# A convolution stage with its last phased chunk moved from the seventh to the eighth, no diagonal taps, and low weight parts formed by accumulating transfers

## The chip, the cores and the metric

The kernel runs on one core of a Trainium2 chip. The core has a matrix engine (TensorE, PE in the profile), a vector engine (VectorE, DVE), a scalar engine (ScalarE, ACT), GpSimd (POOL) and SyncE (SP), which here only issues DMAs; 16 DMA engines move data between HBM and the on-chip memory. Each engine takes its instructions in order, and the instructions of different engines are tied by semaphores. The metric is the device time of one execution in microseconds (us); lower is better.

## The reference

Two layers work on x of 512 tokens by 1024 features. Layer 0 is a Conformer convolution, layer 1 differential attention; each is followed by a SwiGLU feed-forward block and a gated per-layer embedding. The change lies wholly in the convolution of layer 0:

```python
u = rms_norm(h, conv_norm_g[j])
...
a = x @ w_pw1 + b_pw1
u = a[..., :D_MODEL] * jax.nn.sigmoid(a[..., D_MODEL:])
u = lax.conv_general_dilated(u, dw_w[:, None, :], ...)  + dw_b     # 31 causal taps for each feature
u = jax.nn.silu(layer_norm(u, ln_g, ln_b))
return u @ w_pw2 + b_pw2
```

So: a product to 2048 features, a gate, 31 taps along time for each of 1024 features, a layer norm over the features, and a second product.

## The kernel before

**Layout.** Activations lie feature-major: 8 chunks (0 to 7) of 128 features on the partitions by 512 tokens. Products are made to near float32 precision from split operands: a value w is kept as a rounded high part (`hi`) and a low part (`lo` = w − hi), and each product is three matmuls of 128x512 (`mm3`, L183 to L185): low × high, high × low, high × high, in this order.

**Weights.** `weight()` fetches a raw tile of 128x1024 (512 KB, SP's queue, L166), ACT casts it to `hi` (`parts`, L171), and DVE or POOL subtracts to get `lo` (L173). There are two raw buffers and four each for `hi` and `lo`, so that two pairs of weights (gate and linear part of one chunk) fit; the cast of a pair waits until TensorE has finished with the pair two chunks earlier. The weights of chunks 0 and 1 are loaded by hand; those of chunks 2 to 7 come from the two `pairs.append` lines in the loop. Two more, `pw`, hold the weights of the embedding's projection.

**The chunk loop.** For each chunk c TensorE makes two products of 24 matmuls, `pg = half(wg)` and `pa = half(wa)`; DVE scales both by the row norm (L557, L559), ACT takes the sigmoid, and DVE multiplies (L563 or L575). Then come the taps, in one of two ways.

- *Direct* chunks (0, 2, 4, 7): ACT scales shifted copies and POOL adds them (L475, L476; `POOL_TAPS` of them), DVE does the rest as multiply-adds into a PSUM bank (L483 to L487), and both sums are added (L492). Chunk 7 also has an identity matmul and four taps on TensorE with diagonal blocks (L383, L384), added at L494.
- *Phased* chunks (1, 3, 5, 6): the gated input goes to DRAM and comes back with four token phases spread over the partitions (`phased_in`, `pi`: one transfer out, four in, L389 and L393). TensorE does the taps with 8 blocks from `diag` (L406, L412) as 64 matmuls of 128x128 (L422). The result is copied out of PSUM (L435), goes to DRAM and back (`phased_out`, `po`, L437 and L440), gets a remainder (L443) and is finished with the bias and a shift (L449).

**PSUM.** Four banks `mm`, two `sc` and two `tp`. The direct sums and the phased taps of the earlier chunks use `sc`.

**The layer norm.** `moments(c)` squares each finished chunk on ACT (L520) and adds the chunk and its square to two running sums (L523, L526), on POOL for chunks below 6 and on DVE after. `add_moments` turns both sums with TensorE transposes (L256) and reduces them; then come a power on POOL (L636), a spread over the rows, and for each chunk shift, scale, SiLU and a split into `z`. While these run, TensorE is given the eight projections of the embedding (`factor`), issued after the last tap. Then the second product starts (`linear`, L679 to L682).

**Order.** A planner lists the instructions of each engine from simulated times; `tc.issue_after(x)` holds an instruction behind another in that list. The queues run in the listed order whatever the true times are.

Of the kernel before, what the change touches and what calls it, by code (L numbers as in the profile page):

```python
# [49 lines left out]
WARM = 12  # L50
ALONE = (7,)
CUTS = 2


PE_TAPS = (0, 0, 0, 0, 0, 0, 0, 4)
POOL_TAPS = (10, 0, 13, 0, 13, 0, 0, 11)


PHASED = (1, 3, 5, 6)
BEHIND = (6,)  # L60
BEHIND_COPY = {5: -3, 9: -1}
NPH = 4
# [4 lines left out]
for _c in range(NC):  # L67
    if _c in PHASED:
        TAPS += [(_c, g, m) for g in range(NPH) for m in (0, 4)]
    else:  # L70
        TAPS += [(_c, j) for j in range(0, PE_TAPS[_c], 4)]

# [22 lines left out]
def trunk(ctx, tc, xT, pT, wts, diag, dww, vec, rel, lamv, out):  # L95
# [9 lines left out]
    def sb(shape, tag, bufs, dt=F32):  # L105
        uid[0] += 1
        return pool.tile(shape, dt, tag=tag, name=f"{tag}_{uid[0]}", bufs=bufs)
# [60 lines left out]
    def parts(w, cut, eng=V, after=None, behind=None):  # L168
        _, raw, hi, lo = w
        with tc.issue_after(behind.ins) if behind else nullcontext():  # L170
            last_cast[0] = A.copy(hi[:, cut], raw[:, cut])  # L171
        with tc.issue_after(after.ins) if after else nullcontext():
            eng.tensor_tensor(lo[:, cut], raw[:, cut], f(hi[:, cut]), ALU.subtract)  # L173
# [165 lines left out]
    phase_load = [None]  # L339
    late = []  # L340
    rb = None
# [29 lines left out]
    def pe_taps(c):  # L371

        acc = accs[c] = sc() if c < NC - 2 else mm()
        if c in PHASED:
            return phased_taps(c, acc)
        for j in range(PE_TAPS[c]):
            if j % 4 == 0:
                n = min(4, PE_TAPS[c] - j)
                dg = sb([P, 2, 4, P], "C5", 2)[:, 0]
                with tc.issue_after(outs[NC - 3].ins):  # L380
                    nc.sync.dma_start(dg[:, :n], diag[TAPS.index((c, j)), :, :n])
            if j == 0:
                T.matmul(acc, ident, shrow, start=True, stop=False)  # L383
            last_tap[0] = T.matmul(acc, dg[:, j % 4], ups[c][:, j : j + S], start=False, stop=(j == PE_TAPS[c] - 1))  # L384

# [12 lines left out]
    def phased_mats(c):  # L398
        i = TAPS.index((c, 0, 0))
        mats, k = [], 0  # L400
        for g in range(NPH):
            if g < (3 if c == NC - 2 else 2):
                two = []
                for m in range(2):
                    two.append(sb([P, 4, P], f"D{(i + k) % 6}", 1))
                    nc.sync.dma_start(two[m], diag[i + 2 * g + m])  # L406
                    k += 1
            else:
                both_ = sb([P, 2, 4, P], "C5", 2)
                two = both_[:, 0], both_[:, 1]  # L410
                for m in range(2):
                    nc.sync.dma_start(two[m], diag[i + 2 * g + m])  # L412
            mats.append(two)
        return mats
# [12 lines left out]
    def phased_out(c):  # L427

        o = big()
        both_ = sb([P, 2, S], f"B{c}", 1)  # L430
        n = NPH // 2 if c == NC - 2 else NPH
        ways = []
# [11 lines left out]
        y.append(both_[:, 0])  # L444

        def finish():
            if c >= NC - 3:
                more(V)
            return V.scalar_tensor_tensor(  # L449
                both_[:, 0].rearrange(tok, r=NPH), both_[:, 1].rearrange("p (r n) -> p n r", r=NPH), col("dw_b", c),  # L450
                shrow.rearrange(tok, r=NPH), ALU.add, ALU.add,
            )

        if c < NC - 3:
            more(G)
        late.append(finish)
        if c < NC - 3:
            late.pop()()

    def other_taps(c):  # L460
        if c in PHASED:
            return phased_out(c)
        up, acc = ups[c], accs[c]
        tap = lambda j: up[:, j : j + S]
        a, b = PE_TAPS[c], PE_TAPS[c] + POOL_TAPS[c]
        alone = c in ALONE
        pacc = wk()
        for j in range(a, b):
            if j == a:
                A.activation(pacc, tap(j), AF.Identity, scale=wt(c, j), bias=col("dw_b", c))  # L470
            else:
                pr = sb([P, S], f"C{2 + j % 2}", 2)
                behind = [m for m in BEHIND_COPY if m <= j - a] if alone else []
                with tc.issue_after(copies[BEHIND_COPY[behind[-1]]].ins) if behind else nullcontext():
                    A.activation(pr, tap(j), AF.Copy, scale=wt(c, j))  # L475
                last_pool[0] = G.tensor_tensor(pacc, pacc, pr, ALU.add)  # L476
        yc = sb([P, 2, S], f"B{c}", 1)
        if c == 0:
            sums["acc"] = yc[:, 1]
        yc = yc[:, 0]  # L480
        sum_ = sc() if alone else acc
        if c == 0 or alone:
            V.tensor_scalar(sum_, tap(b), wt(c, b), None, ALU.mult)  # L483
        else:
            V.scalar_tensor_tensor(sum_, tap(b), wt(c, b), shrow, ALU.mult, ALU.add)
        for j in range(b + 1, KW):
            last_sum = V.scalar_tensor_tensor(sum_, tap(j), wt(c, j), sum_, ALU.mult, ALU.add)  # L487
            if c == NC - 1 and j == b + 12:
                with tc.issue_after(last_sum.ins):
                    late.pop(0)()  # L490
        with tc.issue_after(last_sum.ins) if alone else nullcontext():
            last_add[0] = V.tensor_tensor(yc, sum_, pacc, ALU.add)  # L492
        if alone:
            last_add[0] = V.tensor_tensor(yc, acc, yc, ALU.add)  # L494
        y.append(yc)
# [6 lines left out]
    last_moment = [None]  # L502
    last_add = [None]
    last_sum = [None]
    last_square = [None]
    last_mean = [None]
    copies = []
    last_pool = [None]

    def moments(c):  # L510
# [7 lines left out]
        sq = wk()  # L518
        with tc.issue_after(last_out[0].ins) if c == NC - 3 else nullcontext():
            last_square[0] = A.activation(sq, y[c], AF.Square)  # L520
        eng = G if c < NC - 2 else V
        if c > 1:
# [12 lines left out]
    for c in range(NC):  # L535
        wa, wg = pairs[c]
        if c == 0:
            pg, pa = first_halves(wa, wg)
            norm.factors()
            rb = norm.rows()  # L540
            pairs.append((weight(), weight())[::-1])
            pair_loads.append(loaded[0])
            ph = pfeatures(0, [(sb([P, S], t, 2, F32R), sb([P, S], t, 2, F32R)) for t in ("wth", "wtl")], norm.spread)
        if 1 < c < NC - 1:
            pairs.append((weight(), weight(load_behind=phase_load[0] if c + 1 in BEHIND else None))[::-1])
            pair_loads.append(loaded[0])
# [29 lines left out]
        if c == NC - 1:  # L576
            other_taps(c - 2)
            pe_taps(c - 1)
        if c > 0 and c != NC - 2:
            other_taps(c - 1)  # L580
        if c == 1:
            moments(0)
        elif c > 3:
            moments(c - 3)
    pe_taps(NC - 1)
    other_taps(NC - 1)
    with tc.issue_after(last_pool[0].ins):
        moments(NC - 3)
    with tc.issue_after(last_square[0].ins):
        A.activation(sb([P, 8], "lam", 1), vt[:, :8], AF.Silu)  # L590
    with tc.issue_after(last_add[0].ins):
        last_add[0] = late.pop()()
    with tc.issue_after(last_add[0].ins):
        sq = moments(NC - 1)
        V.scalar_tensor_tensor(sums["acc"], sq, NC * EPS, sums["acc"], ALU.add, ALU.add)
        moments(NC - 2)

# [25 lines left out]

    pw = [weight(eng=G), weight(eng=G)]
    vs = sb([P, P // 2], "v8", 2)[:, :12]
    for m in range(4):
        factor(last_tap, bank=(mm, mm, mm, sc)[m])
    factor(last_product, copied, between=add_moments)
# [17 lines left out]
    with tc.manual_schedule(engines={V.engine, A.engine}):  # L646
        for c in range(NC + 1):
            if c < NC:
# [5 lines left out]
                z_hi.append(A.copy(z[c][0], y[c]))  # L654
                if c < 3:
                    copied.pop()()
                if c < 2:
                    factor(last_product, copied, (sc, mm)[c])
            if c >= 1:
# [34 lines left out]
    def add_conv(m, acc):  # L694
# [4 lines left out]
        {"eng": G},  # L699
        {"behind": last_square[0], "after": last_pow[0], "eng": G, "load_behind": backs[NC - 2]},  # L700
        {"behind": last_square[0], "after": scaled[1], "load_behind": backs[NC - 2]},
    )
# [550 lines left out]
def _layout(a):  # L1253
# [43 lines left out]
    f = np.arange(FG)  # L1297
    for i, (c, *at) in enumerate(TAPS):
        if c not in PHASED:
            for k in range(min(4, PE_TAPS[c] - at[0])):  # L1300
                diag[i, np.arange(P), k, np.arange(P)] = dw[at[0] + k, c]
            continue
        g0, m0 = at
        for k in range(4):
# [46 lines left out]
```

## Time and profile before

| | us |
|---|---|
| median of 3 runs | 1224.14 |
| lowest, highest | 1223.39, 1225.11 |
| the profiled execution | 1225.47 |
| its span, first to last instruction | 1223.7 |

The profile shows one execution. "Busy" is the time in which an engine had an instruction running; matmuls are pipelined, so that their rows overlap, and a busy TensorE is not one at its peak. A row of the timeline has start, length, engine, line and tiles; a bracket gives the idle time before it and what ended it. The line of a helper such as `mm3` or `parts` stands for many uses. Numbered chunks in the text go from 0 to 7, so that the "eighth chunk" is chunk 7.

### The profile page before, as it was taken

What the parts mean: (1) busy time and instruction counts of PE and PEld (TensorE: products, weight loads), DVE (VectorE), ACT (ScalarE), POOL (GpSimd) and SP (SyncE); (2) the same over time, 40 slices, a digit from 0 to 9 for tenths busy, and PEclk for the clock granted to TensorE, in tenths of its full rate; (3) what the DMA queues carried; (4) which work ended last, traced back from release to release, by engine and by line L of the source; (5) the groups of instructions that cost most, each with busy time, mean ns of one, the idle gap of its engine ahead of it and who ended that gap; (6) DMA issues with size and microseconds to landing.
All of it is one profiled execution on the core that took longest, in us unless ns stands there. A gap on an engine that the chain in (4) does not pass through costs nothing.

```text
span 1223.7 us, 18446 instructions
## 1 busy us (share of the span) xinstructions
PE 1215.3 (99%) x7080; PEld 1072.7 (88%) x7080; DVE 897.1 (73%) x1442; ACT 623.2 (51%) x1039; POOL 279.3 (23%) x238
## 2 busy tenths in 40 slices
PE   9999999999999999999999999999999999999998
PEld 7888788898999899888888989888898999899887
DVE  6999957965698458668668879647865687568668
ACT  6764645432355235446566779635442355235443
POOL 0879421000000000042626544131000000000120
PEclk9999999999999999999999999999999999999999
DMA  8655232663567444243222214412654577353241
GB/s 285 216 177 157 93 121 71 187 165 111 125 170 185 141 106 123 84 145 96 76 92 78 78 55 128 138 59 79 182 163 122 136 173 190 105 138 94 78 139 69
DMA packets 60056, 156.96 MB, mean 128 GB/s; under 512 B 6336, under 2 KB 11200, under 8 KB 59968
## 3 DMA queue, kind: packets, MB, share of 16 engines
q1 hardware_dynamic: 53632, 136.20, 34.9%
q0 software_dynamic: 4608, 16.78, 8.3%
q10 hardware_dynamic: 1728, 2.80, 0.8%
q8 instruction: 55, 0.90, 0.3%
q14 instruction: 33, 0.27, 0.1%
HBM read 150.52 MB, written 4.19 MB: 126 GB/s over the span
## 4 chain that ended last, share of the span: by engine, by line
PE 88%; DVE 5%; DMA 3%; issue 1%; POOL 1%; ACT 1%; SPq 0%; DVEq 0%; POOLq 0%; ACTq 0%
PE mm L183 23%; PE mm L184 23%; PE mm L185 23%; PE tp L185 2%; PE tp L184 2%; PE tp L183 2%; PE sc L184 2%; PE sc L185 2%; PE sc L183 2%; PE mm L1119 1%; DVE wlo L173 1%; DMA C<-in_wts 1%; POOL wk L476 1%; DVE sc L487 1%; DMA wraw<-in_wts 1%
## 5 line engine op out<-in xcount | busy, mean ns | idle before, releaser
L183 PE MATMUL mm<-A,wlo 128*128 128x512 f32 (+1 forms) x816 | 277.0, 342 | 0.5 <-DVE wlo L775 0.5
L184 PE MATMUL mm<-A,whi 128*128 128x512 f32 (+1 forms) x816 | 276.8, 340 | 0.5 <-DVE A L198 0.5
L185 PE MATMUL mm<-A,whi 128*128 128x512 f32 (+1 forms) x816 | 276.9, 340 | 0.0
L171 ACT CAST whi<-wraw 128x1024 fp32r<-128x1024 f32 (+2 forms) x142 | 143.4, 1019 | 206.3 <-PE mm L185 88.1
L173 DVE TENSOR_TENSOR wlo<-wraw,whi 128x1024 fp32r<-128x1024 f32 (+2 forms) x135 | 171.7, 1275 | 54.5 <-ACT whi L171 54.4
L183 PEld LDWEIGHTS mm<-A,wlo 128*128 128x128 f32 x816 | 154.8, 190 | 18.1 <-PE sc L185 0.6
L184 PEld LDWEIGHTS mm<-A,whi 128*128 128x128 f32 x816 | 154.8, 190 | 17.7 <-DVE A L198 0.9
L185 PEld LDWEIGHTS mm<-A,whi 128*128 128x128 f32 x816 | 154.8, 190 | 16.6
L184 PE MATMUL mm<-B,whi 128*128 128x512 f32 (+1 forms) x384 | 147.5, 385 | 0.0
L185 PE MATMUL mm<-B,whi 128*128 128x512 f32 (+1 forms) x384 | 147.4, 385 | 0.0
L183 PE MATMUL mm<-B,wlo 128*128 128x512 f32 (+1 forms) x384 | 145.3, 386 | 0.0
L782 POOL DMA_DIRECT2D C<-in_wts x32 | 27.9, 873 | 506.3 <-DVE h L893 134.8
L224 POOL TENSOR_TENSOR acc<-acc,wk 128x512 f32<-128x512 f32 x34 | 55.8, 1640 | 215.3 <-ACT wk L222 107.4
L185 PEld LDWEIGHTS mm<-B,whi 128*128 128x128 f32 x384 | 72.1, 188 | 14.4
L183 PEld LDWEIGHTS mm<-B,wlo 128*128 128x128 f32 x384 | 72.2, 188 | 13.9
L184 PEld LDWEIGHTS mm<-B,whi 128*128 128x128 f32 x384 | 72.2, 188 | 13.7
L184 PE MATMUL mm<-wlo,A 128*128 128x512 f32 (+1 forms) x224 | 81.6, 367 | 0.0
L183 PE MATMUL mm<-whi,A 128*128 128x512 f32 (+1 forms) x224 | 80.9, 366 | 0.0
L185 PE MATMUL mm<-whi,A 128*128 128x512 f32 (+1 forms) x224 | 80.4, 362 | 0.0
L893 DVE TENSOR_TENSOR h<-mm,h 128x512 f32<-128x512 f32 x48 | 32.9, 687 | 63.5 <-PE mm L185 63.5
L250 POOL TENSOR_TENSOR r<-v,mhalf 128x8 f32<-128x8 f32 (+1 forms) x30 | 45.3, 1511 | 123.3 <-DVE v L248 122.5
L476 POOL TENSOR_TENSOR wk<-wk,C 128x512 f32<-128x512 f32 x43 | 63.4, 1479 | 13.5 <-ACT C L475 10.8
(322 smaller groups left out, 2749.6 us busy)
## 6 DMA issues: line engine op xcount, KB each, us to landing
wraw<-in_wts SPq DMA_DIRECT2D x161, 512.0 KB, 3.7
C<-in_wts SPq DMA_DIRECT2D x32, 512.0 KB, 4.5
C<-in_wts POOLq DMA_DIRECT2D x32, 512.0 KB, 6.0
bias<-in_wts SPq DMA_DIRECT2D x32, 256.0 KB, 3.3
wraw<-in_wts SPq DMA_DIRECT2D x16, 384.0 KB, 3.1
D<-in_diag SPq DMA_DIRECT2D x18, 256.0 KB, 4.9
C<-in_diag SPq DMA_DIRECT2D x15, 256.0 KB, 5.6
h<-in_xT SPq DMA_DIRECT2D x8, 256.0 KB, 5.2
```

The source lines that it names most:

```text
L171: last_cast[0] = A.copy(hi[:, cut], raw[:, cut])
L173: eng.tensor_tensor(lo[:, cut], raw[:, cut], f(hi[:, cut]), ALU.subtract)
L183: T.matmul(acc, al, bh, start=first, stop=False)
L184: T.matmul(acc, ah, bl, start=False, stop=False)
L185: return T.matmul(acc, ah, bh, start=False, stop=last)
L224: self.last = eng.tensor_tensor(self.acc, self.acc, sq, ALU.add)
L250: last_pow[0] = G.tensor_tensor(r[:, :n], v[:, :n], mhalf[:, :n], ALU.pow)
L476: last_pool[0] = G.tensor_tensor(pacc, pacc, pr, ALU.add)
L487: last_sum = V.scalar_tensor_tensor(sum_, tap(j), wt(c, j), sum_, ALU.mult, ALU.add)
L782: nc.gpsimd.dma_start(q, wts[i + 2].rearrange("p (a s) -> p a s", a=2), accum_op=ALU.add)
L893: V.tensor_tensor(h[m], acc, h[m], ALU.add)
L1119: T.matmul(o, wt[:, k * P : (k + 1) * P], val[hd, k], start=(k == 0), stop=(k == qb))
```

## The change

- The phased chunks are 1, 3, 5 and 7; chunk 6 becomes a direct one with 13 taps on ACT and POOL and 18 on DVE. No chunk has diagonal taps on TensorE.
- The weights of chunks 2 to 7 and the two `pw` weights get their low part in a new way (`eng=None`): ACT writes −hi into `lo`, and a DMA from POOL's queue adds the raw weight to it straight from HBM.
- POOL adds chunk 6 to the running sums. The calls at the end come in another order, five projections instead of four are issued straight after the last tap, and several hand-set orders go.

```diff
-ALONE = (7,)
...
-PE_TAPS = (0, 0, 0, 0, 0, 0, 0, 4)
-POOL_TAPS = (10, 0, 13, 0, 13, 0, 0, 11)
-PHASED = (1, 3, 5, 6)
+POOL_TAPS = (10, 0, 13, 0, 13, 0, 13, 0)
+PHASED = (1, 3, 5, 7)
...
     def parts(w, cut, eng=V, after=None, behind=None):
...
             last_cast[0] = A.copy(hi[:, cut], raw[:, cut])
+        if eng is None:
+            A.activation(lo[:, cut], hi[:, cut], AF.Copy, scale=-1.0)
+            nc.gpsimd.dma_start(lo[:, cut], wts[w[0], :, cut].bitcast(F32R), accum_op=ALU.add)
+            return
...
     def pe_taps(c):
-        acc = accs[c] = sc() if c < NC - 2 else mm()
+        acc = accs[c] = sc() if c < NC - 1 else mm()
         if c in PHASED:
-            return phased_taps(c, acc)
-        for j in range(PE_TAPS[c]):
...
-                T.matmul(acc, ident, shrow, start=True, stop=False)
-            last_tap[0] = T.matmul(acc, dg[:, j % 4], ups[c][:, j : j + S], start=False, stop=(j == PE_TAPS[c] - 1))
+            phased_taps(c, acc)
...
     def phased_out(c):
-        n = NPH // 2 if c == NC - 2 else NPH
+        n = NPH // 2 if c == NC - 1 else NPH
...
+        more(G if c < NC - 3 else V)
+        V.scalar_tensor_tensor(
+            both_[:, 0].rearrange(tok, r=NPH), both_[:, 1].rearrange("p (r n) -> p n r", r=NPH), col("dw_b", c),
+            shrow.rearrange(tok, r=NPH), ALU.add, ALU.add,
+        )
...
     def moments(c):
-        with tc.issue_after(last_out[0].ins) if c == NC - 3 else nullcontext():
+        with tc.issue_after(copies[-2].ins) if c == NC - 3 else nullcontext():
-        eng = G if c < NC - 2 else V
+        eng = G if c < NC - 1 else V
...
-            pairs.append((weight(), weight())[::-1])
+            pairs.append((weight(eng=None), weight(eng=None))[::-1])
...
-            pairs.append((weight(), weight(load_behind=phase_load[0] if c + 1 in BEHIND else None))[::-1])
+            pairs.append((weight(eng=None), weight(eng=None, load_behind=phase_load[0] if c + 1 in BEHIND else None))[::-1])
...
         if c == NC - 1:
             other_taps(c - 2)
-            pe_taps(c - 1)
...
+    moments(NC - 2)
     pe_taps(NC - 1)
     other_taps(NC - 1)
-    with tc.issue_after(last_pool[0].ins):
-        moments(NC - 3)
+    moments(NC - 3)
...
-    with tc.issue_after(last_add[0].ins):
-        last_add[0] = late.pop()()
-    with tc.issue_after(last_add[0].ins):
-        sq = moments(NC - 1)
-        V.scalar_tensor_tensor(sums["acc"], sq, NC * EPS, sums["acc"], ALU.add, ALU.add)
-        moments(NC - 2)
+    sq = moments(NC - 1)
+    V.scalar_tensor_tensor(sums["acc"], sq, NC * EPS, sums["acc"], ALU.add, ALU.add)
...
-    pw = [weight(eng=G), weight(eng=G)]
+    pw = [weight(eng=None), weight(eng=None)]
...
-    for m in range(4):
-        factor(last_tap, bank=(mm, mm, mm, sc)[m])
+    for m in range(5):
+        factor(last_tap, bank=(mm, mm, mm, sc, sc)[m])
...
-                if c < 3:
+                if c < 2:
                     copied.pop()()
-                if c < 2:
-                    factor(last_product, copied, (sc, mm)[c])
+                if c < 1:
+                    factor(last_product, copied, mm)
...
-        {"behind": last_square[0], "after": last_pow[0], "eng": G, "load_behind": backs[NC - 2]},
-        {"behind": last_square[0], "after": scaled[1], "load_behind": backs[NC - 2]},
+        {"behind": last_square[0], "after": last_pow[0], "eng": G, "load_behind": backs[NC - 1]},
+        {"behind": last_square[0], "after": scaled[1], "load_behind": backs[NC - 1]},
```

More of the change, by code (lines that the diff above doesn't have):

```diff
@@ L50 @@
 WARM = 12
-ALONE = (7,)
 CUTS = 2
-PE_TAPS = (0, 0, 0, 0, 0, 0, 0, 4)
-POOL_TAPS = (10, 0, 13, 0, 13, 0, 0, 11)
-PHASED = (1, 3, 5, 6)
+POOL_TAPS = (10, 0, 13, 0, 13, 0, 13, 0)
+PHASED = (1, 3, 5, 7)
 BEHIND = (6,)
-BEHIND_COPY = {5: -3, 9: -1}
 NPH = 4
@@ L69 @@
         TAPS += [(_c, g, m) for g in range(NPH) for m in (0, 4)]
-    else:
-        TAPS += [(_c, j) for j in range(0, PE_TAPS[_c], 4)]
 KDUP = "G"
@@ L339, in trunk @@
     phase_load = [None]
-    late = []
     rb = None
@@ L371, in pe_taps @@
     def pe_taps(c):
-        acc = accs[c] = sc() if c < NC - 2 else mm()
+        acc = accs[c] = sc() if c < NC - 1 else mm()
         if c in PHASED:
-            return phased_taps(c, acc)
-        for j in range(PE_TAPS[c]):
[L377 to L383, printed above, removed]
-            last_tap[0] = T.matmul(acc, dg[:, j % 4], ups[c][:, j : j + S], start=False, stop=(j == PE_TAPS[c] - 1))
+            phased_taps(c, acc)
     def phased_in(c, src):
@@ L401, in phased_mats @@
         for g in range(NPH):
-            if g < (3 if c == NC - 2 else 2):
+            if g < (3 if c == NC - 1 else 2):
                 two = []
@@ L444, in phased_out @@
         y.append(both_[:, 0])
[L446 to L458, printed above, removed]
+        more(G if c < NC - 3 else V)
[3 more added lines that the diff above has]
+        )
     def other_taps(c):
@@ L462, in other_taps @@
             return phased_out(c)
-        up, acc = ups[c], accs[c]
+        up, acc = ups[c], accs.get(c)
         tap = lambda j: up[:, j : j + S]
-        a, b = PE_TAPS[c], PE_TAPS[c] + POOL_TAPS[c]
-        alone = c in ALONE
+        b = POOL_TAPS[c]
         pacc = wk()
-        for j in range(a, b):
-            if j == a:
+        for j in range(b):
+            if j == 0:
                 A.activation(pacc, tap(j), AF.Identity, scale=wt(c, j), bias=col("dw_b", c))
@@ L472, in other_taps @@
                 pr = sb([P, S], f"C{2 + j % 2}", 2)
[L473 to L476, printed above, removed]
+                A.activation(pr, tap(j), AF.Copy, scale=wt(c, j))
+                G.tensor_tensor(pacc, pacc, pr, ALU.add)
         yc = sb([P, 2, S], f"B{c}", 1)
@@ L480, in other_taps @@
         yc = yc[:, 0]
-        sum_ = sc() if alone else acc
-        if c == 0 or alone:
-            V.tensor_scalar(sum_, tap(b), wt(c, b), None, ALU.mult)
+        if c == 0:
+            V.tensor_scalar(acc, tap(b), wt(c, b), None, ALU.mult)
         else:
-            V.scalar_tensor_tensor(sum_, tap(b), wt(c, b), shrow, ALU.mult, ALU.add)
+            V.scalar_tensor_tensor(acc, tap(b), wt(c, b), shrow, ALU.mult, ALU.add)
         for j in range(b + 1, KW):
[L487 to L494, printed above, removed]
+            V.scalar_tensor_tensor(acc, tap(j), wt(c, j), acc, ALU.mult, ALU.add)
+        V.tensor_tensor(yc, acc, pacc, ALU.add)
         y.append(yc)
@@ L502, in trunk @@
     last_moment = [None]
-    last_add = [None]
     last_sum = [None]
     last_square = [None]
+    copies = []
     last_mean = [None]
-    copies = []
-    last_pool = [None]
     def moments(c):
@@ L584, in trunk @@
             moments(c - 3)
+    moments(NC - 2)
     pe_taps(NC - 1)
     other_taps(NC - 1)
-    with tc.issue_after(last_pool[0].ins):
-        moments(NC - 3)
-    with tc.issue_after(last_square[0].ins):
+    moments(NC - 3)
+    with tc.issue_after(copies[-1].ins):
         A.activation(sb([P, 8], "lam", 1), vt[:, :8], AF.Silu)
-    with tc.issue_after(last_add[0].ins):
-        last_add[0] = late.pop()()
-    with tc.issue_after(last_add[0].ins):
-        sq = moments(NC - 1)
-        V.scalar_tensor_tensor(sums["acc"], sq, NC * EPS, sums["acc"], ALU.add, ALU.add)
-        moments(NC - 2)
+    sq = moments(NC - 1)
+    V.scalar_tensor_tensor(sums["acc"], sq, NC * EPS, sums["acc"], ALU.add, ALU.add)
     pp = []
@@ L1297, in _layout @@
     f = np.arange(FG)
[L1298 to L1303, printed above, removed]
+    for i, (c, g0, m0) in enumerate(TAPS):
         for k in range(4):
```

## The prediction

> **What bounds the kernel now.** I read the page's busy shares first, then TensorE's waits, then windows over the convolution, then the timeline of its end.
>
> ```profile
> span 1223.7 us, 18446 instructions
> PE 1215.3 (99%) x7080; PEld 1072.7 (88%) x7080; DVE 897.1 (73%) x1442; ACT 623.2 (51%) x1039; POOL 279.3 (23%) x238
> PE tp L256 <- DVE acc L523: 1.2, 1, 1.2
> 20.00:30.00 10.00, 10.00 (x48) 7.94 (x47) 5.23 (x8) 3.14 (x5) 1.18 (x2) 1.00 0.86 303
> 30.00:40.00 10.00, 9.99 (x45) 8.24 (x45) 9.96 (x13) 9.70 (x14) 5.51 (x5) 1.00 0.85 299
> 40.00:80.00 40.00, 40.00 (x241) 35.21 (x240) 39.29 (x43) 24.42 (x36) 32.91 (x24) 1.00 0.55 175
> 80.00:120.00 40.00, 40.00 (x221) 34.70 (x220) 39.22 (x52) 20.68 (x31) 36.88 (x27) 1.00 0.52 162
> ```
>
> The window columns are stretch, its length, then busy time of PE, weight load, DVE, ACT and POOL, granted clock (1.00), DMA share and GB/s. PE is never idle in the convolution's first 120 us, although DVE is full (39.3 of 40 us) and POOL nearly so: both run behind PE without holding it. PE's longest wait in the whole program is 1.2 us, for the transposes of the layer norm's sums. So PE's own work is the floor, and relief of DVE pays only where PE then waits less. The end of the convolution:
>
> ```profile
> 110.69 3.73 PE L422 MATMUL sc<-C,D 128*128 128x128 f32 x32
> 117.83 5.52 PE L422 MATMUL mm<-C,D 128*128 128x128 f32 x48
> 124.97 1.02 PE L383 MATMUL mm<-shrow,ident 128*128 128x512 f32 x2
> 128.87 0.80 PE L183 MATMUL mm<-wth,wlo 128*128 128x512 f32 x1
> 136.74 0.66 PE L256 MATMUL tp<-ident,acc 128*128 128x128 f32 x4 [1.16 <-DVE acc L523]
> 137.34 0.66 PE L256 MATMUL tp<-ident,B 128*128 128x128 f32 x4
> 143.59 0.39 PE L679 MATMUL mm<-A,whi 128*128 128x512 f32 x1
> 142.58 0.62 ACT L654 CAST A<-B 128x512 fp32r<-128x512 f32 x1
> ```
>
> Start, length, instruction. Chunks are numbered 0 to 7. PE ends chunk 7's products at 110.69, does chunk 5's phased taps (7.14 us), chunk 6's (117.83 to 124.97, 7.14 us), the identity and diagonal taps (124.97 to 128.87, 3.90 us), projections, the two groups of transposes, more projections, and the second pointwise product from 143.59. Its first operand's cast ends at 142.58 + 0.62 = 143.20.
>
> **The change, part by part.**
>
> *Removed from PE:* the identity and four diagonal taps, 3.90 us. With the 1.16 us wait that makes 5.06 us, the most this change can give while PE stays the floor.
>
> *The tail becomes a chain.* The projections follow the last tap in program order (they are issued after `last_tap`), and the last tap is now chunk 7's phased one, whose input goes to DRAM and back. Chunk 6 makes that trip now:
>
> ```profile
> 106.53 1.20 DVE L563 SCALAR_TENSOR_TENSOR big<-big,vec,big 128x512 f32<-128x512 f32 x1
> 107.75 0.34 SPq L389 DMA_DIRECT2D pi<-big  x1
> 109.75 1.74 SPq L393 DMA_DIRECT2D C<-pi  x4
> C<-pi SPq DMA_DIRECT2D x8, 64.0 KB, 2.0
> L559 DVE TENSOR_TENSOR big<-mm,rb 128x512 f32<-128x512 f32 x8 | 5.4, 680 | 0.0
> 125.18 0.65 ACT L435 COPY big<-mm 128x256 f32<-128x256 f32 x2 [2.23 <-PE mm L422]
> 127.28 1.75 SPq L440 DMA_DIRECT2D B<-po  x4
> B<-po SPq DMA_DIRECT2D x8, 64.0 KB, 1.9
> L443 DVE TENSOR_TENSOR B<-B,rest 128x240 f32<-128x240 f32 x2 | 2.3, 1154 | 0.0
> L449 DVE SCALAR_TENSOR_TENSOR B<-B,vec,shrow 128x512 f32<-128x512 f32 x4 | 5.1, 1282 | 0.0
> L520 ACT ACTIVATE wk<-B 128x512 f32<-128x512 f32 x7 | 4.3, 627 | 5.8 <-DVE B L449 3.2 <-DVE B L494 1.8 <-DVE B L492 0.7
> L595 DVE SCALAR_TENSOR_TENSOR B<-wk,B 128x512 f32<-128x512 f32 x1 | 0.7, 681 | 0.0
> ```
>
> From the end of the gated input (106.53 + 1.20 = 107.73) to the last landing: the fourth load starts at 109.75 + three quarters of 1.74 = 111.06, plus 2.0 gives 113.1, so 5.4 us. For chunk 7, from 110.69: L559 0.68, the gate 1.20, signals 0.2 (estimate), trip 5.4: 118.2. In between SP also issues the diagonal blocks for chunk 7, waiting for chunk 5's taps to free their buffers; I add 0.5 us (estimate; zero to 1.5, about the time of four such issues): 118.7. Chunk 5's taps, the only work left to PE, end at 117.83: **PE idles 0.9 us** where it did not. Taps: 118.7 + 7.14 = 125.8. Return: from 124.97 to the last landing (127.28 + 1.31 + 1.9 = 130.5) it is 5.5 us now, so 131.3. L443 1.15 and L449 1.28: 133.8. Square 0.63 with a signal (0.15), then L595 0.68: the second transposes start at 135.2, against 137.34. From there to the first operand's cast end it is 143.20 − 137.34 = 5.9 us: **product at 141.1–141.2 against 143.59, 2.4 us sooner.** PE's account agrees: 3.90 + 1.16 less, new idle of 0.9 ahead of the taps, some 0.9 ahead of the transposes and 0.6 ahead of the product: 2.7.
>
> *Moved to the direct way:* chunk 6 has 45 − 43 = 2 more POOL adds and two more DVE taps than chunk 7 had, less L494 and two of DVE's moment sums, which go to POOL. It starts two products of 5.46 us (below) before 110.69, at about 100, and need only be done before 133. I cost it at nothing. If POOL ended it after 127.5, the two sums of chunk 6 and then of chunk 5 (four POOL additions of some 1.5 us, L476's mean below, behind L492) would be later than the chain above.
>
> *Low parts of 14 weights.* DVE loses 12 subtractions and POOL two; ACT gains 14 casts, POOL 14 DMA issues:
>
> ```profile
> L173 DVE TENSOR_TENSOR wlo<-wraw,whi 128x1024 fp32r<-128x1024 f32 x10 | 17.7, 1768 | 0.0
> L476 POOL TENSOR_TENSOR wk<-wk,C 128x512 f32<-128x512 f32 x43 | 63.4, 1479 | 13.5 <-ACT C L475 10.8
> L171 ACT CAST whi<-wraw 128x1024 fp32r<-128x1024 f32 x14 | 14.6, 1041 | 4.9 <-DMA wraw<-in_wts 4.7
> L782 POOL DMA_DIRECT2D C<-in_wts x32 | 27.9, 873 | 506.3 <-DVE h L893 134.8
> q0 software_dynamic: 4608, 16.78, 8.3%
> 40.00:50.00 10.00, 10.00 (x71) 9.22 (x70) 9.96 (x10) 6.77 (x11) 9.61 (x7) 1.00 0.34 89
> C<-in_wts POOLq DMA_DIRECT2D x3, 512.0 KB, 8.4
> C<-in_wts POOLq DMA_DIRECT2D x32, 512.0 KB, 6.0
> 19.72 1.05 ACT L171 CAST whi<-wraw 128x1024 fp32r<-128x1024 f32 x1 [0.49 <-DMA wraw<-in_wts]
> 30.37 1.05 ACT L171 CAST whi<-wraw 128x1024 fp32r<-128x1024 f32 x1
> 30.04 0.49 PE L183 MATMUL mm<-A,wlo 128*128 128x512 f32 x1
> 77.95 0.48 PE L183 MATMUL mm<-A,wlo 128*128 128x512 f32 x1
> ```
>
> DVE gains 17.7 us in this stage and two subtractions before it; off PE's path that is worth nothing, except that DVE should then be prompt at 110.69, as the tail above assumes. ACT takes 14 × 1.04 = 14.6 us into a stage where it is busy 45 of 80 us. POOL takes 14 × 0.87 = 12.2 us, plus the adds and sums of chunk 6, less two subtractions; its queue is in order, so an issue that waits for ACT's second cast holds the L476 adds behind it, then ACT's scaled taps (their buffers) and DVE's last sum. PE has no direct need of these.
>
> The price lies in when the low part lands, because each product's first matmul reads it. The accumulating queue cost 8.3% × 1223.7 / 32 = 3.2 us of all 16 engines for each transfer. Four low parts (chunks 2 and 3) fall into 20–40 us, where DMA is at 0.86 and 0.85: 17.1 us used, 12.8 more wanted, 20 there. Later ones have 5 to 20 us to spare against a share near 0.55. The landing, 6.0 us in the median of the run, was 8.4 in the median of three at 225–246 us. Chunk 2's gate weight: cast ends 20.77, second cast 21.8, issue at 22.0, landed 30.4 by the 8.4, while PE wants it at 30.04. Chunk 3's: cast from 30.37, second cast ends 32.5, landed 40.9, wanted at 40.95 (two products after 30.04; the last six run from 77.95 to 110.69, so 5.46 us each). Both lie on the edge: **I take a stall of 0.8 us**, from 0 (landing of 8.0 or less) to 5 (13 us, all of the missing 10 us of DMA time shared between the two queues). A stall of the first shifts the second's need too, so they do not add.
>
> On this the Trainium skill can be weighed. Its page "DMA: Bandwidth & Descriptors", section "Anatomy of one DMA — SWDGE (gpsimd) path", gives about 2.0 us plus bytes over 436 GB/s for a transfer from this queue, by my estimate 3.2 us for 512 KB. By that the sum would have no stall; the rows here say 6.0 and 8.4, and I go by them. The same page, "Issuing engines are not separate DMA queues", says that transfers from all queues interleave on the same 16 engines, which speaks against this change: were the queues apart, the landing would stay at 6.0 and the stall at 0. No row here yet shows the early window overfull.
>
> *Sum:* 2.4 − 0.8 = 1.6 us sooner. The profiled execution took 1225.47 us, 1.77 around its span, and lies 1.33 above the median of 1224.14; the difference is carried to the median: **1222.5 us**.
>
> **Rivals.**
>
> 1. *Clean:* no stall, no time lost on SP's queue (0.5), and L449 falls from 1.28 towards the 0.68 that L595 takes for the same size (0.6). Gain 2.4 + 0.5 + 0.6 = 3.5, at most the floor of 5.06: about 1220.6. For it: DVE has slack and POOL has no subtraction left there until the power.
> 2. *Short landing:* the tail as forecast, but every low part lands in 8.0 us or less, as the run's median of 6.0 has it. The stall falls away: 1224.14 − 2.4 = 1221.7. This is also where the fixed price of the Trainium skill's page "DMA: Bandwidth & Descriptors" would lead.
> 3. *A bank:* the scratch banks in PSUM are two. Chunk 6's sum takes one earlier, so chunk 5's taps on PE wait for chunk 4's sum:
>
> ```profile
> 112.51 0.69 DVE L492 TENSOR_TENSOR B<-sc,wk 128x512 f32<-128x512 f32 x1
> ```
>
> It is read last at 112.51 + 0.69 = 113.2, now 2.5 us too late for 110.69. The relief of 17.7 us should bring it ten or more microseconds forward; if chunk 6's taps are put ahead of chunk 4's, it does not, and PE loses 2.5 to 7: about 1227.
>
> 4. *Slower, the early DMA window.* With DMA demand of 30 us in 20, the accumulates land after 12 to 14 us and the raw weights and diagonal blocks beside them are late too. The stall is landing − 8.0; it outweighs the 2.4 us from a landing of 10.4 us on, and by 0.2% from 12.9 on. At 13.5: 1224.14 − 2.4 + 5.5 = 1227.2. Against it: the window after it, 40–50 us, has a share of 0.34, so that what is not urgent can slip there.
>
> That the change doesn't do what it says is hardly open: five matmul groups go, and nothing else on PE is added.
>
> **How the numbers follow.** About 0.2%, 2.45 us, is what a measurement of this kernel can tell from no change. Forecast (gain 0.3 to 2.9): 0.45. Clean: 0.20. Short landing: 0.12, on the edge of 0.2%, half to each side. Bank: 0.08. Early DMA: 0.15. Faster: 0.20 + 0.06 + 0.07 of the forecast = 0.33. Slower: 0.08 + 0.15, and 0.01 of the forecast = 0.24. Same: the rest of the forecast, 0.37, and 0.06 = 0.43. The range for 8 in 10 goes from 1219.5, near the floor, to 1228.5, above both slower cases; the forecast's own is 1221.2 to 1223.8.
>
> **What would show it.** Right: no L383 and L384; PE idle for about 1 us ahead of the last L422 group, waiting for C<-pi; the second transposes 24.5 us after the end of chunk 7's products (26.65 now); L173 on DVE gone from 30–100 us; wlo landings of 8 us in 20–40 us with PE waiting at most a microsecond at the first L183 of chunk 2 or 3. Wrong: PE waiting several microseconds on a DMA before 60 us (rival 4); PE's chunk-5 taps waiting for L492 (rival 3); POOL's adds ending after 127 us, with the moment sums of POOL released last; or an order of instructions that moves chunk 5's taps ahead of chunk 7's products, so that nothing is left beside the trip.

## The result and the profile after

| | before | after |
|---|---|---|
| median, us | 1224.21 (5 runs) | 1243.55 (5 runs) |
| lowest, highest | 1223.39, 1225.11 | 1241.96, 1244.58 |
| ratio, 95% interval | | 1.0156 [1.0141, 1.017] |
| span of the profiled execution | 1223.7 | 1240.2 |
| mean granted clock | 1.000 | 0.993 |

The changed kernel is slower by 19.3 us in the median; the two profiled executions, 1225.47 and 1241.96 us, are 16.5 us apart, and the rows below account for these 16.5. The forecast was 1222.5, with a range up to 1228.5. Lines have moved: the casts are L166 and L168, the accumulating transfer L169, the matmuls of `mm3` L182 to L184, the phased taps L411, their way back L424 to L435, the running sums L491 and L494, the products' scaling and gate L525 to L531, and the second product L642.

The page of the changed kernel first (queue rows: packets, MB, share of 16 engines; issue rows: count, size, median us to landing):

```profile
PE 1220.2 (98%) x7070; PEld 1077.2 (87%) x7070; DVE 881.2 (71%) x1429; ACT 637.3 (51%) x1055; POOL 285.1 (23%) x254
q0 software_dynamic: 6624, 24.12, 11.6%
wlo<-in_wts POOLq DMA_DIRECT2D x14, 512.0 KB, 7.6
D<-in_diag SPq DMA_DIRECT2D x18, 256.0 KB, 7.6
C<-in_diag SPq DMA_DIRECT2D x14, 256.0 KB, 8.8
```

TensorE is still "98% busy" and even busier in microseconds (1220.2 against 1215.3) with ten instructions fewer; that share says nothing of where the time went. Where it went is in the windows and the timeline of the first 165 us. Windows of the changed kernel (columns as in the prediction):

```profile
20.00:30.00 10.00, 9.24 (x44) 7.10 (x43) 3.39 (x7) 7.55 (x10) 4.61 (x5) 1.00 0.99 294
30.00:40.00 10.00, 8.73 (x32) 7.07 (x33) 6.36 (x10) 6.64 (x10) 7.00 (x6) 0.83 1.05 298
40.00:50.00 10.00, 10.00 (x46) 8.29 (x45) 9.75 (x14) 10.00 (x15) 7.61 (x7) 1.00 0.96 292
50.00:60.00 10.00, 10.00 (x76) 9.19 (x75) 6.32 (x9) 7.33 (x11) 9.19 (x10) 1.00 1.03 262
```

The last column but one is the DMA share: full (about 1) for 40 us, where before it was 0.86, 0.85, in 40–50 0.34 and in 50–60 0.77. The column ahead of it is the granted clock: 0.83 in 30–40, where it was 1.00.

TensorE's timeline in the changed kernel (a bracket is the idle time before the row, and what ended it):

```profile
31.27 0.47 PE L182 MATMUL mm<-A,wlo 128*128 128x512 f32 x1 [2.03 <-DMA wlo<-in_wts]
32.67 0.63 PE L184 MATMUL mm<-A,whi 128*128 128x512 f32 x1
33.10 0.63 PE L182 MATMUL mm<-A,wlo 128*128 128x512 f32 x1
36.14 0.39 PE L184 MATMUL mm<-A,whi 128*128 128x512 f32 x1
36.37 0.39 PE L182 MATMUL mm<-A,wlo 128*128 128x512 f32 x1
...
78.71 5.44 PE L411 MATMUL sc<-C,D 128*128 128x128 f32 x32 [3.55 <-DMA C<-pi]
109.18 0.47 PE L182 MATMUL mm<-A,wlo 128*128 128x512 f32 x1 [1.01 <-DMA wlo<-in_wts]
116.75 0.47 PE L182 MATMUL mm<-A,wlo 128*128 128x512 f32 x1 [1.89 <-DMA wlo<-in_wts]
...
123.90 3.73 PE L411 MATMUL sc<-C,D 128*128 128x128 f32 x32
135.56 8.44 PE L411 MATMUL mm<-C,D 128*128 128x128 f32 x48 [4.36 <-DMA C<-pi]
145.54 0.48 PE L182 MATMUL mm<-wth,wlo 128*128 128x512 f32 x1
160.41 0.50 PE L642 MATMUL mm<-A,whi 128*128 128x512 f32 x1 [0.88 <-ACT A L617]
```

The second product starts at 160.41 instead of 143.59: 16.8 us, so the whole loss of the span (16.5) lies in the convolution stage. The projections start at 145.54 instead of 128.87, 16.7 us later, and behind them both kernels take the same (14.9 and 14.7). So the 16.7 us are to be found ahead of 145.54, and the rows give them:

- **Waits, 12.8 us**: 2.03 + 3.55 + 1.01 + 1.89 + 4.36.
- **A slow clock behind four of the five waits, 7.7 us.** At 32.67 one matmul follows the other after 0.43 us, at 36.14 after 0.23. That lasts some 3.4 us behind three of the waits and nearly 6 us behind the last. The 32 taps at 78.71 take 5.44 instead of 3.73 us; the last 64 taps take 145.54 − 135.56 = 10.0 instead of 7.14. The four cost 1.6, 1.7, 1.6 and 2.8 us.
- **Work removed, 3.9 us**: the diagonal taps are gone, as forecast. 12.8 + 7.7 − 3.9 = 16.6.

Why was chunk 7's input so late? Rows of the other engines in the changed kernel, in order of time (SPq rows are issues; L461 and L463 from 122.81 on are direct taps of chunk 6):

```profile
98.66 1.75 SPq L429 DMA_DIRECT2D B<-po  x4
103.47 2.97 DVE L435 SCALAR_TENSOR_TENSOR B<-B,vec,shrow 128x512 f32<-128x512 f32 x1 [7.55 <-POOL B L432]
115.42 0.72 ACT L526 ACTIVATE big<-big,vec 128x512 f32<-128x512 f32 x1 [3.93 <-DVE big L525]
117.44 0.88 POOL L169 DMA_DIRECT2D wlo<-in_wts  x1 [2.89 <-ACT wlo L168]
119.68 0.69 DVE L464 TENSOR_TENSOR B<-sc,wk 128x512 f32<-128x512 f32 x1 [4.29 <-POOL wk L453]
122.81 0.74 DVE L461 SCALAR_TENSOR_TENSOR sc<-C,C,shrow 128x512 f32<-128x512 f32 x1
123.59 3.13 DVE L463 SCALAR_TENSOR_TENSOR sc<-C,C,sc 128x512 f32<-128x512 f32 x4
126.63 0.68 DVE L527 TENSOR_TENSOR big<-mm,rb 128x512 f32<-128x512 f32 x1
128.32 1.57 DVE L531 SCALAR_TENSOR_TENSOR big<-big,vec,big 128x512 f32<-128x512 f32 x1 [0.35 <-ACT big L526]
129.92 0.33 SPq L378 DMA_DIRECT2D pi<-big  x1
```

Before, the same return of chunk 3 was issued here:

```profile
86.92 1.75 SPq L440 DMA_DIRECT2D B<-po  x4
```

Chunk 3's way back is 11.7 us late: its taps start 7.8 us later on TensorE (78.71 against 70.89), run slower, and their result takes 5.2 instead of 4.0 us to DRAM. DVE, which had been full, stands idle for 7.55 us with its list blocked by that one instruction. Then ACT waits for DVE, POOL's transfer for ACT's cast, and DVE for POOL's last add: each queue is in order, and the lateness goes around. It reaches TensorE too: the two low parts that it waits for at 109.18 and 116.75 belong to chunk 7 and are read 5.8 us after their issue, but they were issued only at 103.38 and 110.98, the first behind the late return in POOL's list. Chunk 7's products end at 123.90, its gate only at 128.32 + 1.57 = 129.9. That is 6.0 us later, where the prediction had 2.1. DVE is no longer idle then: it does chunk 6's taps, which stand in its list ahead of the last scaling (L527) and the gate (L531).

### The profile page after: what moved, and what is told of

Read it like the earlier page. It is cut to its first block, busy times and chain, and to the rows that moved or that the text cites. A ratio compares the mean times of both kernels' runs of the same rounds, so it can differ in the third digit from the quotient of the medians.

```text
span 1240.2 us, 18461 instructions
## 1 busy us (share of the span) xinstructions
PE 1220.2 (98%) x7070; PEld 1077.2 (87%) x7070; DVE 881.2 (71%) x1429; ACT 637.3 (51%) x1055; POOL 285.1 (23%) x254
## 3 DMA queue, kind: packets, MB, share of 16 engines
q0 software_dynamic: 6624, 24.12, 11.6%
## 4 chain that ended last, share of the span: by engine, by line
PE 91%; DMA 3%; DVE 2%; issue 1%; POOL 1%; ACT 1%; SPq 0%; ACTq 0%; DVEq 0%; POOLq 0%
PE mm L182 23%; PE mm L183 23%; PE mm L184 23%; PE tp L184 3%; PE tp L183 3%; PE tp L182 3%; PE sc L183 1%; PE sc L182 1%; PE sc L184 1%; PE mm L1082 1%; DMA D<-in_diag 1%; POOL wk L453 1%; PE sc L1049 1%; PE sc L411 1%; PE sc L1048 1%
## 5 line engine op out<-in xcount | busy, mean ns | idle before, releaser
L182 PE MATMUL mm<-A,wlo 128*128 128x512 f32 (+1 forms) x816 | 277.9, 343 | 5.2 <-DMA wlo<-in_wts 4.9
L184 PE MATMUL mm<-A,whi 128*128 128x512 f32 (+1 forms) x816 | 278.2, 341 | 0.0
L166 ACT CAST whi<-wraw 128x1024 fp32r<-128x1024 f32 (+2 forms) x142 | 143.4, 1018 | 210.0 <-PE mm L184 85.4
L172 DVE TENSOR_TENSOR wlo<-wraw,whi 128x1024 fp32r<-128x1024 f32 (+2 forms) x123 | 151.1, 1232 | 52.2 <-ACT whi L166 52.2
L182 PEld LDWEIGHTS mm<-A,wlo 128*128 128x128 f32 x816 | 155.6, 191 | 23.9 <-DVE big L527 2.4
L184 PEld LDWEIGHTS mm<-A,whi 128*128 128x128 f32 x816 | 155.7, 191 | 17.0
L184 PE MATMUL mm<-B,whi 128*128 128x512 f32 (+1 forms) x384 | 147.4, 385 | 0.0
L182 PE MATMUL mm<-B,wlo 128*128 128x512 f32 (+1 forms) x384 | 145.3, 386 | 0.0
L184 PEld LDWEIGHTS mm<-B,whi 128*128 128x128 f32 x384 | 72.2, 188 | 14.4
L182 PEld LDWEIGHTS mm<-B,wlo 128*128 128x128 f32 x384 | 72.2, 188 | 13.9
L183 PEld LDWEIGHTS mm<-B,whi 128*128 128x128 f32 x384 | 72.2, 188 | 13.8
L182 PE MATMUL mm<-whi,A 128*128 128x512 f32 (+1 forms) x224 | 80.9, 366 | 0.0
L184 PE MATMUL mm<-whi,A 128*128 128x512 f32 (+1 forms) x224 | 80.4, 362 | 0.0
```

What stands on the lines that cost most here:

```text
L182: T.matmul(acc, al, bh, start=first, stop=False)
L183: T.matmul(acc, ah, bl, start=False, stop=False)
L184: return T.matmul(acc, ah, bh, start=False, stop=last)
```

## The experiments

The change has two halves: where the chunks go (phased eighth chunk, no diagonal taps) and how low parts are made. Theory: an overfull DMA in 20–60 us, made by the accumulating transfers, gives the loss. Rival: the new tail loses by itself, with chunk 7's gate behind DVE's taps. Each kernel below computes the whole reference. A difference in us is the ratio's, on 1224 us. In the cuts of code, `...` stands for further lines of the edit.

### Each half by itself

The changed kernel with all low parts subtracted as before:

```diff
-pairs.append((weight(eng=None), weight(eng=None))[::-1])
+pairs.append((weight(), weight())[::-1])          # the second pairs line likewise
-pw = [weight(eng=None), weight(eng=None)]
+pw = [weight(eng=G), weight(eng=G)]
```

> The changed kernel, but all low parts made as before (DVE, and POOL for the two pw weights); the eighth chunk stays phased. Theory D (the 14 accumulating transfers overfill the DMA engines between 20 and 60 us, and everything that crosses DRAM comes late): DMA share back to 0.85 at 30-40 us, no PE wait for wlo, time 1221 to 1227, near the forecast tail's 1221.7. Theory T (the tail: the eighth chunk's trip through DRAM has too little work beside it): PE still waits over 4 us for C<-pi ahead of the last taps, time 1236 or more. Theory A (the extra casts on ACT hold its queue): as D.

Measured: 1235.09 us, 1.0079 [1.0063, 1.0096]. It waits nowhere for a low part. A window of it, TensorE's waits (total, times, longest), and the timeline of DVE and TensorE:

```profile
40.00:60.00 20.00, 20.00 (x123) 17.77 (x121) 19.61 (x24) 12.93 (x19) 19.33 (x14) 1.00 0.58 183
```

```profile
PE mm L411 <- DMA C<-pi: 9.6, 1, 9.6
PE tp L255 <- DVE acc L491: 1.4, 1, 1.4
```

```profile
113.12 2.41 DVE L461 SCALAR_TENSOR_TENSOR sc<-C,C,shrow 128x512 f32<-128x512 f32 x1
115.56 2.34 DVE L463 SCALAR_TENSOR_TENSOR sc<-C,C,sc 128x512 f32<-128x512 f32 x3
119.06 2.15 DVE L531 SCALAR_TENSOR_TENSOR big<-big,vec,big 128x512 f32<-128x512 f32 x1
...
109.77 3.73 PE L411 MATMUL sc<-C,D 128*128 128x128 f32 x32
126.71 8.23 PE L411 MATMUL mm<-C,D 128*128 128x128 f32 x48 [9.64 <-DMA C<-pi]
```

In 40–60 us the DMA is at 0.58 and the clock full, TensorE ends chunk 7's products at 109.77 without a wait, and still 9.7 us are lost: DVE is full, chunk 6's taps stand ahead of chunk 7's gate, and the gate ends at 121.2, 11.4 us after the products. The rival is true too.

The kernel before with the accumulating low parts in all 14 places (`eng=None` at both `pairs` lines and at `pw`):

```diff
         last_cast[0] = A.copy(hi[:, cut], raw[:, cut])
+        if eng is None:
+            A.activation(lo[:, cut], hi[:, cut], AF.Copy, scale=-1.0)
+            nc.gpsimd.dma_start(lo[:, cut], wts[w[0], :, cut].bitcast(F32R), accum_op=ALU.add)
+            return
...
```

> The kernel before, with the 14 low parts made by the sign-turned cast and the accumulating transfer; the seventh chunk stays phased and the diagonal taps stay. Theory D: DMA share near 1 at 20-60 us, PE waits for wlo and C<-pi, 1235 to 1245. Theory T: within 2 us of 1224. Theory A: 1235 or more, with PE's waits led by ACT and not by DMA.

Measured: 1244.24 us, 1.0161 [1.0146, 1.0176]. TensorE's waits in it (total, times, longest):

```profile
PE sc L426 <- DMA C<-pi: 4.2, 1, 4.2
PE mm L187 <- DMA wlo<-in_wts: 3.9, 3, 2.6
PE mm L426 <- DMA C<-in_diag: 3.4, 1, 3.4
PE mm L187 <- DVE big L563: 2.3, 1, 2.3
```

With the old tail the transfers alone cost as much as the whole change. So each half loses alone, 20 and 10 us, and together they lose 19: they share their waits and do not add. Only 3.9 of the 13.8 us of waits are put down to low parts; 7.6 are for the input of a phased chunk and for diagonal blocks, which had been in time before.

### Is it ACT's work or the transfer's, and its source?

The changed kernel, where DVE adds the raw weight to ACT's sign-turned cast, and no transfer is made:

```diff
-nc.gpsimd.dma_start(lo[:, cut], wts[w[0], :, cut].bitcast(F32R), accum_op=ALU.add)
+V.tensor_tensor(lo[:, cut], raw[:, cut], f(lo[:, cut]), ALU.add)
```

> The changed kernel with the sign-turned cast on ACT kept for the 14 low parts, but the raw weight added to it by DVE from the raw tile in place of the accumulating transfer. Theory D: 1221 to 1229, DMA share as before. Theory A: 1236 or more. Theory T: 1236 or more.

Measured: 1234.26 us, 1.0076 [1.0056, 1.0096], the same as without the casts. ACT's 14.6 us of casts cost nothing here, as forecast; beside the transfers they were not tried alone.

The changed kernel, accumulating from the raw tile that is on the chip already, so that HBM isn't read twice:

```diff
-nc.gpsimd.dma_start(lo[:, cut], wts[w[0], :, cut].bitcast(F32R), accum_op=ALU.add)
+nc.gpsimd.dma_start(lo[:, cut], raw[:, cut].bitcast(F32R), accum_op=ALU.add)
```

> The changed kernel with the accumulating transfer reading the raw tile on the chip in place of HBM. If it is the accumulation into the destination that costs: DMA share in 20-60 us stays near 1.0 and the time is 1239 to 1247. If it is the second read of HBM: share 0.85 or less, 1230 to 1237.

Measured: 1241.78 us, 1.0142 [1.0123, 1.016]. TensorE's waits in it:

```profile
PE mm L411 <- DVE sc L463: 7.8, 1, 7.8
PE mm L182 <- DMA wlo<-wraw: 7.4, 4, 3.1
```

The first row names a tap of chunk 6, but that is only the event that came last: the loads of chunk 7's input were issued at 132.47 and the wait ends 3.6 us later, at 136.04, just as in the changed kernel (131.98 and 135.56). The page's row for POOL's queue is the changed kernel's to the digit (11.6% of 16 engines). Sparing the second read of HBM gives back little: it is the accumulating transfer that is dear, wherever it reads from.

### Which of the transfers?

The changed kernel with accumulating low parts only from chunk 4 on, and then only in chunks 2 and 3:

```diff
-pairs.append((weight(eng=None), weight(eng=None, load_behind=...))[::-1])
+low = V if c + 1 < 4 else None      # the other kernel: None if c + 1 < 4 else V
+pairs.append((weight(eng=low), weight(eng=low, load_behind=...))[::-1])
...
```

> The changed kernel, but the low parts of chunks 2 and 3 made by DVE; chunks 4 to 7 and pw by accumulating transfers. Theory D, early window alone to blame: share at 20-40 us back to 0.86, and about 1224 to 1229. Theory D, total demand to blame: 1232 to 1240, with the waits at the later chunks left. Theory T: 1236 or more.

> The changed kernel with accumulating transfers for chunks 2 and 3 alone, the other low parts as before. Theory E: DMA share near 1 at 20-45 us, a PE wait for wlo or C<-pi ahead of 60 us, and 1240 to 1248, 5 us or more above e1's 1235.1. If the later transfers are needed for the loss: within 2 us of e1.

Measured: 1233.13 us, 1.0067 [1.0046, 1.0087], from chunk 4 on; 1238.74 us, 1.0119 [1.0101, 1.0138], in chunks 2 and 3 only. Against 1.0079 with none and 1.0156 with all: the four early ones cost about 5 us on top of the tail, the late ones nothing that can be told (−1.5 us, the intervals overlap), both together 9.4. In the early-only kernel TensorE waits:

```profile
PE mm L411 <- DMA C<-pi: 9.8, 1, 9.8
PE mm L182 <- DMA wlo<-in_wts: 3.9, 2, 2.2
```

The first four bring 3.9 us of stalls and leave the tail's wait as it was. In the kernel from chunk 4 on, the tail's wait is down to 3.5 us, but TensorE waits 2.0 us for a low part and 2.8 for the sums instead. That the later ones cost more behind the early ones than alone fits a DMA that stays full for 40 us; no run separates this further.

The kernel before with accumulating low parts only in chunks 4 to 6 and `pw`, all of which have microseconds to spare:

```diff
+low = None if 4 <= c + 1 <= 6 else V
...
-pw = [weight(eng=G), weight(eng=G)]
+pw = [weight(eng=None), weight(eng=None)]
```

> The kernel before with accumulating transfers only for chunks 4, 5 and 6 and for pw, where DMA had room (share 0.34 to 0.55 from 40 us on, and e3 lost nothing by it). Theory E (only the four early transfers cost): PE waits under 2 us in all, 1222 to 1226. If transfers cost anywhere: PE waits for wlo or C<-pi of 2 us or more and the slow clock behind them, 1228 or more.

Measured: 1230.60 us, 1.0055 [1.0042, 1.0069]. TensorE has one wait, and SP's rows ahead of it show where it comes from:

```profile
110.06 0.34 SPq L393 DMA_DIRECT2D pi<-big  x1
115.98 1.74 SPq L397 DMA_DIRECT2D C<-pi  x4
117.82 1.80 SPq L410 DMA_DIRECT2D D<-in_diag  x4
...
123.44 7.07 PE L426 MATMUL mm<-C,D 128*128 128x128 f32 x48 [5.69 <-DMA D<-in_diag]
```

From the issue of chunk 6's trip to its loads it takes 5.9 us here and took 2.0 before (107.75 to 109.75). The diagonal blocks of the next taps stand behind those loads in SP's list, and TensorE waits 5.69 us for blocks that were issued only at 117.82. No low part is late in this kernel. The price of the transfers is paid by others.

### Can the tail be mended?

The changed kernel with subtracted low parts, and chunk 6's first DVE tap ordered behind chunk 7's gate:

```diff
...
+with tc.issue_after(gates[NC - 1].ins) if c == NC - 2 else nullcontext():
     V.scalar_tensor_tensor(acc, tap(b), wt(c, b), shrow, ALU.mult, ALU.add)
```

> The kernel of e1 (phased eighth chunk, no accumulating transfers), with chunk 6's first vector tap issued behind chunk 7's gate, so that the order on DVE puts the gate ahead. Theory O (the gate comes late because DVE's list has chunk 6's and chunk 4's taps ahead of it: 121.2 in e1, 11.5 us after the products' end): the gate ends by 115, PE's wait for C<-pi falls from 9.6 to 2-4 us with no slow clock behind it, time 1224 to 1229. Theory L (the length of the trip through DRAM itself): the wait stays over 7 us, 1233 or more.

Measured: 1234.07 us, 1.0079 [1.0065, 1.0093]. TensorE's waits:

```profile
PE mm L411 <- DMA C<-pi: 4.2, 1, 4.2
PE tp L255 <- DVE acc L492: 4.1, 1, 4.1
```

The wait for the gate falls from 9.6 to 4.2 us, and the wait for the running sums grows from 1.4 to 4.1, because chunk 6's taps now end at 136.4 us instead of 131.7 and POOL's sum of that chunk comes behind them. The time stays, and the second product starts only 0.4 us sooner: in this order the sums lose what the gate gains.

The same, with the low parts of chunk 7 and of `pw` accumulated to relieve DVE where the DMA has room (a share of 0.49 in 80–100 us and 0.33 in 100–120 without them):

```diff
-pairs.append((weight(), weight(load_behind=...))[::-1])
+low = None if c + 1 == NC - 1 else V
+pairs.append((weight(eng=low), weight(eng=low, load_behind=...))[::-1])
```

> As e7, and the low parts of chunk 7's pair and of pw made by accumulating transfers, so that DVE and POOL are relieved only where DMA has room (share 0.5 after 85 us in e1). Theory O with D (demand in the first 60 us is what the transfers cost): PE's waits under 3 us in all, 1222 to 1227, no later than e7. If transfers cost at any place: later than e7, 1228 to 1234.

Measured: 1234.47 us, 1.0083 [1.0068, 1.0099]; waits of 3.7 and 3.1 us with 0.9 for a low part. Nothing is gained.

### The diagonal taps alone, and the clock

The kernel before without the diagonal taps: two of them go to POOL, two to DVE, and the identity matmul and the add of its bank (L494) go with them.

```diff
-PE_TAPS = (0, 0, 0, 0, 0, 0, 0, 4)
-POOL_TAPS = (10, 0, 13, 0, 13, 0, 0, 11)
+PE_TAPS = (0, 0, 0, 0, 0, 0, 0, 0)
+POOL_TAPS = (10, 0, 13, 0, 13, 0, 0, 13)
...
```

> The kernel before with the identity and diagonal taps alone taken off PE: chunk 7 gets 13 taps on ACT and POOL and 18 on DVE, the seventh chunk stays phased, low parts as before. Theory F (PE's work is the floor): the 3.9 us go, 1220 to 1222. Theory C (the chain of chunk 7's taps on POOL and DVE to the sums sets the end of the stage, and PE's 3.9 us only filled the wait): PE's wait ahead of the transposes grows from 1.2 to 4-7 us, time 1223 to 1229.

Measured: 1229.55 us, 1.0041 [1.0028, 1.0053], so 5 us slower with 3.9 us less work for TensorE. Its rows:

```profile
138.43 1.12 PE L256 MATMUL tp<-ident,acc 128*128 128x128 f32 x4 [7.89 <-DVE acc L523]
141.06 0.63 PE L185 MATMUL mm<-wtl,whi 128*128 128x512 f32 x1
```

The sums are ready 1.7 us later than before (138.43 against 136.74), TensorE waits 7.89 us for them instead of 1.16, and then transposes for 1.12 instead of 0.66 us. To part the wait from the clock, the same kernel with eight matmuls of 128x512 laid into the wait; their result is not used, and the trace shows each as two:

```diff
+warm = tp()
+with tc.issue_after(last_product[0].ins):
+    for _ in range(8):
+        last_product[0] = T.matmul(warm, ones, shrow, start=True, stop=True)
 factor(last_product, copied, between=add_moments)
```

> The kernel of e9 with eight added matmuls of 128x512 (some 6.2 us of PE, result unused) ahead of the transposes of the sums, where PE waited 7.9 us. Theory W (a wait of PE of several us is followed by some 3 us at about half clock, as after each long wait so far): the wait falls to about 2 us, the slow stretch after it is gone or shorter, and the time falls from e9's 1229.6 to 1226-1228.5 although PE does more. If the slow clock costs nothing there: 1229 to 1231, as e9.

Measured: 1226.27 us, 1.0015 [1.0006, 1.0024]. Its rows:

```profile
129.64 7.03 PE L631 MATMUL tp<-shrow,ones 128*128 128x512 f32 x16
138.49 0.66 PE L256 MATMUL tp<-ident,acc 128*128 128x128 f32 x4 [1.13 <-DVE acc L523]
```

The transposes start when they did (138.49 and 138.43), but the kernel is 3.3 us faster than the one without the filler. In 138–141 us the granted clock is 0.50 without the filler and 1.00 with it, and the second product starts at 147.94 and 145.39. So useless work in a wait is worth 3.3 us, at least 2.6 of them through the clock between the transposes and the second product.

Last, what seemed to cost least of each half, in the kernel before: no diagonal taps, accumulating low parts in chunks 4 to 6 and `pw`, and chunk 7 with 10 taps on POOL.

```diff
-POOL_TAPS = (10, 0, 13, 0, 13, 0, 0, 11)
+POOL_TAPS = (10, 0, 13, 0, 13, 0, 0, 10)
...
+low = None if 4 <= c + 1 <= 6 else V
```

> No diagonal taps (as e9), accumulating transfers for chunks 4 to 6 and pw (as e11), and the room on DVE used: chunk 7 has 10 taps on ACT and POOL and 21 on DVE. Theory C (the chain of chunk 7 on POOL and DVE sets the end): POOL ends two adds earlier, DVE has no backlog; the sums' transposes come at 134 to 137 us, and the time is 1220 to 1226. If it does not help: as e9 or later, 1229 or more.

Measured: 1232.96 us, 1.0076 [1.0062, 1.009], with waits of 4.3 us (phased taps) and 3.2 us (sums), both followed by the slow clock. No version tried is faster than the kernel before.

## Why the prediction was wrong

**Right in it.** The diagonal taps are gone and take 3.9 us with them; ACT's casts are free where no transfer follows them; a transfer takes 3.0 us of all 16 engines, forecast 3.2 ((11.6% × 1240.2 − 8.3% × 1223.7) / 14 = 3.0). The landing in 20–60 us is 8.8 us, forecast 8.4. The trip of chunk 7's input, from the gate's end at 129.9 to the taps at 135.56, is 5.7, forecast 5.4. No bank was late (rival 3). TensorE does wait for chunk 7's C<-pi.

**"I take a stall of 0.8 us": mis-sized, and the wrong kind of sum.** The stall at the first low part was 2.03 us, within its 0 to 5; the waits in all were 12.8 us. The text had the demand, 30 us of DMA in 20, and gave it a chance of 0.15 (rival 4) at a price of 3 us. It then asked only of the low parts whether each lands in time, gave the later ones 5 to 20 us to spare, and held that the stalls "do not add" and that what isn't urgent can slip into the window of 0.34. What slipped filled that window and the next, to 0.96 and 1.03. The victims were other transfers: in 20–60 us the blocks of `in_diag` and the trips of the phased chunks lie on the same engines, and the median landing of the diagonal blocks in that stretch went from 6.3 and 5.9 to 10.1 and 13.9 us (4.9 and 5.6 to 7.6 and 8.8 over the whole run). Later low parts came late through POOL's list, and not through their landing. In the kernel before, the accumulating low parts cost 20 us, of whose waits 3.9 are for low parts. The right sum is a backlog over the whole stretch, with everything that lies in it counted as late. Here the trace agrees with the rule of the Trainium skill that the prediction weighed ("DMA: Bandwidth & Descriptors", section "Issuing engines are not separate DMA queues"). The other rule that the prediction took from the Trainium skill (the same page, section "Anatomy of one DMA — SWDGE (gpsimd) path"), 2.0 us and the bytes over 436 GB/s, by my estimate 3.2 us, is not the landing of these: 7.6 us in the median.

**"DVE … should then be prompt at 110.69": false.** The gate ends 6.0 us after the products in the changed kernel and 11.4 us after in the one with subtractions. In the latter DVE is full, and chunk 6's direct taps stand in its list ahead of the gate. In the former they stand there too (122.81 to 126.7); DVE's idle 7.55 and 4.29 us came before, with the list held by a late return. The prediction costed chunk 6's move to the direct way at nothing because the work was not due before 133. It looked at when the taps had to be done, not at where they stand in DVE's list and in front of what.

**"PE's own work is the floor": true, but 3.9 us less of it gave nothing.** The kernel before with only the diagonal taps removed is 5 us slower. The sums' chain was 1.2 us behind TensorE. Four taps moved to DVE and POOL make it 1.7 us later, and TensorE then waits for all that it was spared and more. A wait of 1.2 us is not slack of DVE; it says that two chains end together.

**A term that was missing: the clock.** The prediction read 1.00 in every window and had no price for a wait beyond its length. The four long waits of the changed kernel cost another 7.7 us, 46% of its loss. The filler shows that it is the idle time that does this: with the wait filled, the clock behind it stayed at 1.00.

**What stays open.** How the 9.4 us that the transfers add to the new tail split between the early and the late ones was not separated beyond the two halves above; and whether an order of DVE's list exists in which the eighth chunk's gate and the sums are both in time was tried in one place only.

## What to carry over

Before a transfer is put in place of an engine's work, sum the DMA time of the whole stretch, not the landing of that transfer: in a full window others pay, and in-order queues carry their lateness to engines that have nothing to do with it. When an engine at 99% is relieved, look at the chain that ends just behind it and at what takes the work over. And price a wait of TensorE above about two microseconds at more than its length: the slow clock behind it cost 1.6 to 2.8 us in the changed kernel and up to 3.3 where it was filled.

## What the hardware showed

**The clock falls after a wait.** Over all 14 traces, behind TensorE's waits from 20 us to the second product: after none of the waits up to 1.71 us was the granted clock lower; after 9 of the 13 between 1.89 and 3.50 us it was 0.50; after all 13 from 3.55 to 9.77 us it was 0.50, for 3 us or more, at times nearly 6. The Trainium skill has this in "TensorE: Matmul & The Clock Gate": section "What's actually happening" describes half rate after an idle window of about 3.4 us, a window that runs freely, and full rate after as long a busy one. The 3.4 us that the clock took to recover behind three waits of the changed kernel agree, and that waits of like length differ (1.89 does it, 2.65 in the kernel before with all accumulating parts doesn't) fits the free-running window. But the same page of the Trainium skill, in section "Why this matters for your kernels", allows gaps up to about 3 us, and here 1.89 us is enough. The measurement decides.

**An accumulating transfer is dear from either source.** It takes 3.0 us of all 16 engines for 512 KB, and the same share of them whether it reads HBM or the raw tile on the chip. For comparison, the other large queue of the kernel before takes 1.6 us for as many bytes, by an estimate from its page (34.9% of 1223.7 us for 136.20 MB).
